# A delta-rule layer: the rescaling of the normed stream and the level masks of the triangular inverse move from GpSimd to VectorE

## The chip, the cores and the metric

The kernel runs on one core of one Trainium2 chip. The metric is device microseconds from launch to end on that core. Before the change three timed runs took 2519.2, 2519.74 and 2502.26 us; their median is 2519.2 us. A change of this kernel has to be about 1% to be told from no change.

## The reference

Two transformer blocks follow each other on 512 tokens of width 1024, in float32. The first has a windowed-attention layer (a) and a neighbourhood-attention layer (b), each with a gated feed-forward part, and ends in an RMS norm with the gain `norm_final`. The second puts 16 meta tokens in front (528 tokens from there on) and has a layer (c) with short convolutions and a gated delta rule, a layer (d) with sliding-window attention, and a feed-forward part behind each.

The change lies in layer (c). Two pieces of it matter:

- The stream that enters it: x becomes x · (row factor of the final norm) · (gain per feature). This normed x is the residual that layer (c) adds its result to.
- The delta rule, cut to its core. For each of 4 heads, tokens in chunks, k and q of 128 features, beta and the decay per token:

```
a = strictly lower part of beta * (k k^T) * decay mask
u, w = (I + a)^-1 [ v*beta , k*beta*exp(decay) ]
per chunk: v_new = u - w S ; o = q_dec S + (q k^T * decay mask) v_new ; S = S*g + k_dec^T v_new
```

## The kernel before

Tensors lie transposed, features on partitions and tokens along the free axis, 8 tiles of 128 x 528 for x. Every projection is done with float32 split into a high and a low part (`split`, L429 on ScalarE and L430 on VectorE) and three matmuls per tile (L254 to L256); its results are taken out of PSUM by VectorE (L404), which frees one of three PSUM banks named `mm`. The order of instructions on each engine isn't the order of the source: the framework's scheduler sets it when the kernel is built, and each engine then runs its list strictly in order.

Layer (c) begins with the projections of k. Behind the row factors come the convolutions (`conv_of`, three VectorE passes at L981 per tile) and `stream` (L646), which rescales the 8 tiles of x in place: per tile one multiplication by the gain on GpSimd (L652) and one by the row factor, a 128 x 512 tile r1 (L653). The rescaled tiles are then written to DRAM as the residual (`spill`). They are read back much later.

The delta rule works on 5 chunks (16 tokens, then 4 of 128). `rule` runs the preparation (`prep`) of two chunks side by side and the chain over the state behind them; `weave` interleaves this with the remaining projections of the layer (q, v, gate, z), which are the filling work for TensorE. `prep` inverts I + a by doubling: in blocks of 64, a level l takes the part of a that the mask `lev[l]` (128 x 64, made once by GpSimd) leaves, called `am`:

- level 0: `am` at L1591 on GpSimd, then x^T = identity - am at L1592 on VectorE, then a transposition on TensorE (L1605 for the upper, L1603 for the lower half), copied out by ScalarE (L1607).
- levels 1 to 5 (1 to 3 for the first chunk): `am` at L1615 on GpSimd, TensorE product with x (L1619), ScalarE copy (L1622), TensorE product (L1626), VectorE subtraction from x^T (L1627), and again the transposition.

So `am` of a level depends on `ac` (L1588) and the mask alone, not on the level before. There are 5 executions of L1591 and 23 of L1615. Other GpSimd work of the stage are the decay terms (L1523, L1551, L1557, L1559), q times the decay (L1661), the assembly of the inverse (L1636, L1638) and a sum of the output norm (L1729).

Of the kernel before, what the change touches and what calls it, by code (L numbers as in the profile page):

```python
# [13 lines left out]
ALU = mybir.AluOpType  # L14
# [5 lines left out]
S = 512  # L20
# [40 lines left out]
def bc_head(ap2, n):  # L61

    return ap2.unsqueeze(1).to_broadcast([ap2.shape[0], n, ap2.shape[1]])
# [59 lines left out]
def kernel(ctx: ExitStack, tc: tile.TileContext, stop=None, **a):  # L123
    nc = tc.nc
    V, A, G, PE = nc.vector, nc.scalar, nc.gpsimd, nc.tensor
# [15 lines left out]
    def slot(p="s"):  # L141
        for t, (n, names) in TAGS.items():
            if p in names:
                return sp.tile([P, SW], F32, tag=t, name=nm(p), bufs=n)
        return sp.tile([P, SW], F32, tag="s", name=nm(p), bufs=NSLOT)
# [7 lines left out]
    def bank(tag):  # L153
        tag, pool, bufs = psx[tag]
        return pool.tile([P, 512], F32, tag="ps" + tag, name=nm("ps" + tag), bufs=bufs)
# [48 lines left out]
    def gcol(key, k):  # L204
        return ncol[:, norm_at[key] + k:norm_at[key] + k + 1]
# [261 lines left out]
    def rows(c, cm=None):  # L467


        nw, m = c.shape[1], c.shape[2]  # L470
        rb = wk("rb")
        rv = rb[:, :nw * P].rearrange("p (w m r) -> p w m r", w=nw, m=m)
        V.tensor_copy(rv, c.unsqueeze(3).to_broadcast([P, nw, m, P // m]))
        ps = bank("s")
        for w in range(nw):
            PE.transpose(ps[:, w * P:(w + 1) * P], rb[:, w * P:(w + 1) * P], ident)
        if cm is None:
            return ps, None
        rm = tp.tile([P, P], F32, tag="rbm", name=nm("rbm"), bufs=2)
        V.tensor_copy(rm[:NMETA].rearrange("p (m r) -> p m r", m=m), cm.unsqueeze(2).to_broadcast([NMETA, m, P // m]))  # L480
        pm = bank("s")
        PE.transpose(pm[:, :NMETA], rm[:NMETA, :], ident[:NMETA, :NMETA])
        return ps, pm
# [105 lines left out]
    class FirstNorm:  # L589
# [56 lines left out]
        def stream(self, X):  # L646
            ps, _ = rows(self.y[:, 5:].unsqueeze(2))
            r1 = slot("r1")
            A.copy(r1[:, :S], ps)
            for k in range(KC):  # L650
                x = X[k][:, self.R]
                G.tensor_scalar(x, x, gcol(("norm_final", None), k), None, ALU.mult)  # L652
                G.tensor_tensor(x, x, r1[:, :S], ALU.mult)  # L653

    def load_rows_of(src, ntok, mid=None):

# [756 lines left out]
    def layer_c(X):  # L1413
# [9 lines left out]
        lev = []  # L1423
# [102 lines left out]
        def prep(c):  # L1526
            o, C = CH[c]
# [49 lines left out]
            at, ac = slot("at"), slot("ac")  # L1577
            V.tensor_tensor(at[:C, :n4], brow[:C, :n4], E[:C, :n4], ALU.mult)

            B = min(C, H)  # L1580
# [3 lines left out]
            def vb4(t, p=slice(0, C)):  # L1584
                return t[p, :4 * B].rearrange("p (h i) -> p h i", h=4)
# [2 lines left out]
                V.tensor_tensor(vb4(ac, q), v4(kk)[q, :, q], v4(at)[q, :, q], ALU.mult)  # L1588
            xt, x = slot("xt"), slot("xi")
            am = slot("am")  # L1590
            G.tensor_tensor(vb4(am), vb4(ac), bc_head(lev[0][:C, :B], 4), ALU.mult)  # L1591
            V.tensor_tensor(vb4(xt), bc_head(identc[:C, :B], 4), vb4(am), ALU.subtract)  # L1592
            if C > B:
                a2 = slot("a2")
# [3 lines left out]
            def turned(qs):  # L1598
                px = bank("s")
                for q in qs:  # L1600
                    for h in hb:
                        if q.start:
                            PE.matmul(px[q, h], xt[q, h], ident[q, q], start=True, stop=True)  # L1603
                        else:
                            PE.transpose(px[q, h], xt[q, h], ident[q, q])  # L1605
                r = slice(qs[0].start, qs[-1].stop)
                A.copy(x[r, :4 * B], px[r, :4 * B])  # L1607
# [3 lines left out]
            l = 1  # L1611
            while (1 << l) < B:
                last = (2 << l) == B
                am = slot("am")
                G.tensor_tensor(vb4(am), vb4(ac), bc_head(lev[l][:C, :B], 4), ALU.mult)  # L1615
                py = bank("s")
                for q in parts:
                    for h in hb:
                        PE.matmul(py[q, h], am[q, h], x[q, h], start=True, stop=True)  # L1619
                yield 0.8  # L1620
                y = slot("y")
                A.copy(y[:C, :4 * B], py[:C, :4 * B])  # L1622
                pzt = bank("s")
                for q in parts:
                    for h in hb:
                        PE.matmul(pzt[q, h], y[q, h], xt[q, h], start=True, stop=True)  # L1626
                V.tensor_tensor(xt[:C, :4 * B], xt[:C, :4 * B], pzt[:C, :4 * B], ALU.subtract)  # L1627
                yield 0.8
                if not last:
                    turned(parts)  # L1630
                    yield 0.43
                l += 1
# [117 lines left out]
        def rule():  # L1750
            todo, gens, nxt, ch = list(range(len(CH))), [], 0, None
            while nxt < len(CH) or after:
                while todo and len(gens) < 2:
                    if todo[0] < 2:
                        for c in range(min(2, len(CH)) if todo[0] == 0 else 0):
                            decay_rows(c)
                    else:
                        decay_rows(todo[0])
                    gens.append(prep(todo.pop(0)))
                for g in list(gens):  # L1760
                    try:
                        yield next(g)
                    except StopIteration:
                        gens.remove(g)
                for g in list(after):
                    try:
                        yield next(g)
                    except StopIteration:
                        after.remove(g)
                if ch is None and nxt in state:  # L1770
                    ch = chain(nxt)
                if ch is not None:
                    try:
                        yield next(ch)
                    except StopIteration:
                        ch = None
                        nxt += 1
# [436 lines left out]
```

## Time and profile before

| what | value |
|---|---|
| median of three runs | 2519.2 us |
| the profiled execution's own time | 2514.64 us |
| its span, first to last instruction | 2512.9 us |
| TensorE (PE) matmul busy | 2457.7 us, 98% |
| VectorE (DVE) busy | 1831.0 us, 73% |
| ScalarE (ACT) busy | 1199.2 us, 48% |
| GpSimd (POOL) busy | 278.5 us, 11% |
| granted TensorE clock, mean | 0.980 |

The granted clock is a share of 2.4 GHz; where a stretch shows 0.50, TensorE ran at 1.2 GHz. A TensorE that is busy at 0.50 does half the work in the same busy time. Layer (c) lies between about 1178 and 1530 us of the span. In the views, "idle before" names the time that an engine stood idle before an instruction and what ended that time.

### The profile page before, as it was taken

The page shows a single profiled execution, that of the slowest core. Times are in us where ns is not written, and L with a number is a line of the kernel's source. Part 1 is how long each engine was busy: PE and PEld are TensorE (multiplying, and loading weights), DVE is VectorE, ACT ScalarE, POOL GpSimd, SP SyncE. Part 2 cuts the span into 40 slices and gives each one's busy share as a digit, 9 for nine tenths or more (in the row PEclk, how much of TensorE's full clock was granted, in tenths as well). Part 3 has the DMA queues.
Part 4 walks back from the last instruction along what each step waited for, and adds up shares of the span by engine and source line. Part 5 has one row for each costly group of instructions (what it writes and reads, how often), then busy time and mean ns, then how long its engine had stood idle before and what let it go on. Part 6 is the DMA issues. An engine that isn't in the chain of part 4 may idle for free.

```text
span 2512.9 us, 44394 instructions
## 1 busy us (share of the span) xinstructions
PE 2457.7 (98%) x17518; PEld 2223.6 (88%) x17518; DVE 1831.0 (73%) x3520; ACT 1199.2 (48%) x2199; POOL 278.5 (11%) x403
## 2 busy tenths in 40 slices
PE   8999999999999999999999999999999999999999
PEld 6787789998887799998888899899999978889998
DVE  6875767778765878777836446978887776788885
ACT  4764444445555444445423224445544664445553
POOL 3120300003130200003312220200000000100000
PEclk9999999999999999999969999999999999999999
DMA  6142224344232223333311113123324312223332
GB/s 194 43 142 83 78 74 124 111 151 134 77 102 64 63 89 114 105 106 102 108 31 38 35 51 120 55 82 112 98 89 144 68 40 81 68 88 102 101 97 84
DMA packets 345445, 229.19 MB, mean 91 GB/s; under 512 B 54435, under 2 KB 335444, under 8 KB 345236
## 3 DMA queue, kind: packets, MB, share of 16 engines
q1 hardware_dynamic: 342372, 217.59, 29.3%
q0 software_dynamic: 2864, 8.77, 1.1%
q8 instruction: 137, 2.24, 0.4%
q14 instruction: 72, 0.59, 0.1%
HBM read 214.10 MB, written 13.74 MB: 91 GB/s over the span
## 4 chain that ended last, share of the span: by engine, by line
PE 44%; DVE 4%; issue 2%; POOL 1%; ACT 0%; POOLq 0%; DVEq 0%
PE mm L254 10%; PE mm L255 10%; PE mm L256 10%; PE pss L254 1%; PE pss L255 1%; PE pss L256 1%; PE pss L1619 1%; PE pso L2046 1%; PE pss L1626 1%; PE pso L254 1%; PE pso L255 1%; PE pso L256 1%; DVE xb L430 1%; PE pss L1603 1%; PE pss L2031 1%
## 5 line engine op out<-in xcount | busy, mean ns | idle before, releaser
L429 ACT ACTIVATE hi<-raw 128x1024 fp32r<-128x1024 f32 (+1 forms) x458 | 475.5, 1040 | 533.9 <-PE pss L255 256.1
L430 DVE TENSOR_TENSOR lo<-raw,hi 128x1024 fp32r<-128x1024 f32 (+1 forms) x458 | 560.1, 1224 | 135.9 <-ACT hi L429 132.5
L254 PE MATMUL mm<-xh,hi 128*128 128x264 f32 (+3 forms) x1168 | 390.1, 334 | 8.6 <-ACT xh L508 3.2
L255 PE MATMUL mm<-xl,hi 128*128 128x264 f32 (+3 forms) x1168 | 381.4, 327 | 0.6 <-DVE xl L509 0.5
L256 PE MATMUL mm<-xh,lo 128*128 128x264 f32 (+3 forms) x1168 | 379.3, 325 | 0.0
L254 PE MATMUL mm<-xb,hi 128*128 128x256 f32 (+2 forms) x1152 | 328.0, 285 | 18.5 <-ACT xb L429 8.2
L256 PE MATMUL mm<-xb,lo 128*128 128x256 f32 (+2 forms) x1152 | 328.2, 285 | 3.0 <-DVE lo L430 3.0
L255 PE MATMUL mm<-xb,hi 128*128 128x256 f32 (+2 forms) x1152 | 327.5, 284 | 0.3
L256 PE MATMUL mm<-ah,lo 128*128 128x512 f32 (+1 forms) x880 | 307.7, 350 | 0.5 <-DVE lo L430 0.5
L255 PE MATMUL mm<-al,hi 128*128 128x512 f32 (+1 forms) x880 | 307.9, 350 | 0.1
L254 PE MATMUL mm<-ah,hi 128*128 128x512 f32 (+1 forms) x880 | 307.7, 351 | 0.2
L254 PEld LDWEIGHTS mm<-xh,hi 128*128 128x128 f32 x1168 | 226.2, 194 | 32.5 <-issue 6.9
L688 DVE TENSOR_TENSOR xr<-mm,xr 128x512 f32<-128x512 f32 (+1 forms) x288 | 158.2, 557 | 128.5 <-PE mm L256 128.3
L255 PEld LDWEIGHTS mm<-xl,hi 128*128 128x128 f32 x1168 | 226.1, 194 | 17.3 <-DVE xl L509 2.4
L254 PEld LDWEIGHTS mm<-xb,hi 128*128 128x128 f32 x1152 | 219.3, 190 | 23.5 <-ACT xb L429 9.1
L256 PEld LDWEIGHTS mm<-xh,lo 128*128 128x128 f32 x1168 | 225.7, 193 | 16.2 <-issue 0.5
L256 PEld LDWEIGHTS mm<-xb,lo 128*128 128x128 f32 x1152 | 219.8, 191 | 4.0 <-DVE lo L430 3.9
L255 PEld LDWEIGHTS mm<-xb,hi 128*128 128x128 f32 x1152 | 219.2, 190 | 3.4 <-DVE xb L430 0.9
L256 PEld LDWEIGHTS mm<-ah,lo 128*128 128x128 f32 x880 | 165.4, 188 | 23.2 <-DVE lo L430 0.8
L254 PEld LDWEIGHTS mm<-ah,hi 128*128 128x128 f32 x880 | 165.3, 188 | 19.5 <-ACT ah L429 0.9
L255 PEld LDWEIGHTS mm<-al,hi 128*128 128x128 f32 x880 | 165.5, 188 | 18.8 <-DVE al L430 1.0
L255 PE MATMUL pss<-xb,hi 128*128 128x256 f32 (+2 forms) x576 | 163.3, 284 | 1.8 <-DVE xb L430 1.8
(527 smaller groups left out, 5194.1 us busy)
## 6 DMA issues: line engine op xcount, KB each, us to landing
raw<-in_w_gate_up_dram SPq DMA_DIRECT2D x140, 256.0 KB, 3.0
raw<-in_ffn_w_up_dram SPq DMA_DIRECT2D x140, 256.0 KB, 3.0
raw<-in_w_down_dram SPq DMA_DIRECT2D x40, 512.0 KB, 3.3
raw<-in_ffn_w_down_dram SPq DMA_DIRECT2D x40, 512.0 KB, 3.4
raw<-in_mix_w_in_dram SPq DMA_DIRECT2D x28, 512.0 KB, 3.7
raw<-in_w_in_b_dram SPq DMA_DIRECT2D x20, 512.0 KB, 3.7
a<-in_w_gate_up_dram SPq DMA_DIRECT2D x36, 256.0 KB, 3.3
a<-in_ffn_w_up_dram SPq DMA_DIRECT2D x36, 256.0 KB, 2.9
```

What stands on the lines that cost most here:

```text
L254: PE.matmul(ps, r32(hi), r32(xh), start=first, stop=False, skip_group_check=more)
L255: PE.matmul(ps, r32(hi), r32(xl), start=False, stop=False, skip_group_check=more)
L256: PE.matmul(ps, r32(lo), r32(xh), start=False, stop=last, skip_group_check=more)
L429: A.activation(r32(dst_h), src, AF.Copy)
L430: V.tensor_tensor(r32(dst_l), src, dst_h, ALU.subtract)
L688: V.tensor_tensor(X[j][:, o:o + n], ps[:, :n], X[j][:, o:o + n], ALU.add)
L1603: PE.matmul(px[q, h], xt[q, h], ident[q, q], start=True, stop=True)
L1619: PE.matmul(py[q, h], am[q, h], x[q, h], start=True, stop=True)
L1626: PE.matmul(pzt[q, h], y[q, h], xt[q, h], start=True, stop=True)
L2031: PE.transpose(pt[:, d:d + P], pb[:, c:c + P], ident)
L2046: PE.matmul(po[64 * hh:64 * hh + 64, b * P:(b + 1) * P], vt[b + j][:, kv * 64:kv * 64 + 64], PT[:, (2 * hh + j) * P:(2 * hh + j + 1) * P], ...
```

## The change

`stream` multiplies each tile once, on VectorE, by the gain (a scalar per partition) and by r1 in the same instruction. The mask products `am` of all levels are issued on VectorE, with the same operands. Nothing else is edited. Behind L652 the lines of the changed kernel have numbers lower by one (L653 is gone).

```diff
             for k in range(KC):
                 x = X[k][:, self.R]
-                G.tensor_scalar(x, x, gcol(("norm_final", None), k), None, ALU.mult)
-                G.tensor_tensor(x, x, r1[:, :S], ALU.mult)
+                V.scalar_tensor_tensor(x, x, gcol(("norm_final", None), k), r1[:, :S], ALU.mult, ALU.mult)
...
             am = slot("am")
-            G.tensor_tensor(vb4(am), vb4(ac), bc_head(lev[0][:C, :B], 4), ALU.mult)
+            V.tensor_tensor(vb4(am), vb4(ac), bc_head(lev[0][:C, :B], 4), ALU.mult)
             V.tensor_tensor(vb4(xt), bc_head(identc[:C, :B], 4), vb4(am), ALU.subtract)
...
                 am = slot("am")
-                G.tensor_tensor(vb4(am), vb4(ac), bc_head(lev[l][:C, :B], 4), ALU.mult)
+                V.tensor_tensor(vb4(am), vb4(ac), bc_head(lev[l][:C, :B], 4), ALU.mult)
```

The order on the engines changes with it, from where GpSimd began to rescale x (1160 us) to the end of the delta rule. Ahead of that and behind it the lists are the same.

First place, VectorE where the convolutions of k end; L404 takes a projection out of a PSUM bank. Before:

```order
L981 SCALAR_TENSOR_TENSOR qkv_12656<-cg_12492,cwcol,qkv_12656 128x525
L404 TENSOR_TENSOR cg_12699<-mm_12726,rs_12634 128x264
L404 TENSOR_TENSOR cg_12758<-mm_12759,rs_12634 128x264
L981 SCALAR_TENSOR_TENSOR qkv_12752<-cg_12699,cwcol,qkv_12752 128x527
L981 SCALAR_TENSOR_TENSOR qkv_12752<-cg_12699,cwcol,qkv_12752 128x526
L981 SCALAR_TENSOR_TENSOR qkv_12752<-cg_12699,cwcol,qkv_12752 128x525
L430 TENSOR_TENSOR lo_12894<-raw_12891,hi_12893 128x1024
L404 TENSOR_TENSOR cg_12758<-mm_12785,rs_12634 128x264
```

With the change eight passes of `stream` (now L652; the last two are shown) stand between the sixth pass of the convolutions and the next L404:

```order
L652 SCALAR_TENSOR_TENSOR xc_12374<-xc_12374,ncol,r_12669 128x512
L652 SCALAR_TENSOR_TENSOR xc_12403<-xc_12403,ncol,r_12669 128x512
L404 TENSOR_TENSOR cg_12691<-mm_12718,rs_12634 128x264
L404 TENSOR_TENSOR cg_12750<-mm_12751,rs_12634 128x264
L404 TENSOR_TENSOR cg_12750<-mm_12777,rs_12634 128x264
```

The two L404 that followed the sixth convolution pass now follow `stream`, and the third one has moved up to them, ahead of the next convolution.

Second place, VectorE at the head of the inverse of the first two chunks. Before (the products `am` are on the list of GpSimd):

```order
L1588 TENSOR_TENSOR ac_13227<-pss_13143,at_13226 16x64
L981 SCALAR_TENSOR_TENSOR qkv_13200<-cg_13049,cwcol,qkv_13200 128x526
L1592 TENSOR_TENSOR xt_13230<-lev_12449,am_13232 16x64
L981 SCALAR_TENSOR_TENSOR qkv_13200<-cg_13049,cwcol,qkv_13200 128x525
L1578 TENSOR_TENSOR at_13244<-pss_13187,E_13164 128x512
L404 TENSOR_TENSOR cg_13541<-mm_13603,rs_12634 128x264
L1588 TENSOR_TENSOR ac_13245<-pss_13186,at_13244 64x256 x2
L404 TENSOR_TENSOR cg_13668<-mm_13669,rs_12634 128x264
L1592 TENSOR_TENSOR xt_13249<-lev_12449,am_13251 128x256
L1596 TENSOR_TENSOR a_13254<-pss_13186,at_13244 64x256
L430 TENSOR_TENSOR lo_13895<-raw_13892,hi_13894 128x1024
```

With the change (L1590 is level 0's `am`, L1591 the subtraction):

```order
L1590 TENSOR_TENSOR am_13224<-ac_13219,lev_12449 16x64
L980 SCALAR_TENSOR_TENSOR qkv_13192<-cg_13041,cwcol,qkv_13192 128x525
L1591 TENSOR_TENSOR xt_13222<-lev_12449,am_13224 16x64
L404 TENSOR_TENSOR cg_13533<-mm_13595,rs_12634 128x264
L404 TENSOR_TENSOR cg_13660<-mm_13661,rs_12634 128x264
L1577 TENSOR_TENSOR at_13236<-pss_13179,E_13156 128x512
L1587 TENSOR_TENSOR ac_13237<-pss_13178,at_13236 64x256 x2
L430 TENSOR_TENSOR lo_13887<-raw_13884,hi_13886 128x1024
L1590 TENSOR_TENSOR am_13243<-ac_13237,lev_12449 128x256
L404 TENSOR_TENSOR cg_13660<-mm_13710,rs_12634 128x264
L1591 TENSOR_TENSOR xt_13241<-lev_12449,am_13243 128x256
L1595 TENSOR_TENSOR a_13246<-pss_13178,at_13236 64x256
```

One L430 and one L404 now stand between `ac` and the x^T of the 128-token chunk, beside the mask itself. On TensorE the instructions that wait for these x^T have moved back behind filling projections: from the last product of the decay (L1575, 128 x 512) to the first chunk's transposition there were 18 matmuls of projections and are 25 now; from there to the 128-token chunk's (L1605, 64x64) there were 26 and are 45.

Third place, GpSimd at the same point; before, the products `am` of all levels of the two chunks stand one behind the other:

```order
L1559 TENSOR_TENSOR E_13164<-E_13164,rk_13077 128x512
L1591 TENSOR_TENSOR am_13232<-ac_13227,lev_12449 16x64
L1591 TENSOR_TENSOR am_13251<-ac_13245,lev_12449 128x256
L1615 TENSOR_TENSOR am_13266<-ac_13227,lev_12449 16x64
L1615 TENSOR_TENSOR am_13279<-ac_13245,lev_12449 128x256
```

With the change that list goes from the decay straight to q times the decay and the assembly of the inverse:

```order
L1558 TENSOR_TENSOR E_13156<-E_13156,rk_13069 128x512
L1660 TENSOR_TENSOR qd_13585<-qkv_13035,ed_13120 128x16
L1660 TENSOR_TENSOR qd_13585<-qkv_13192,ed_13120 128x16
L1660 TENSOR_TENSOR qd_13585<-qkv_13380,ed_13120 128x16
L1660 TENSOR_TENSOR qd_13585<-qkv_13515,ed_13120 128x16
L1635 MEMSET xf_13677 64x4x64
```

So nothing on GpSimd stands any more between the decay terms and the first assembly but q times the decay.

## Rows read from the trace of the kernel before

**Rows 1.** The page: busy time by engine (us, share of the span, instructions).

```profile
PE 2457.7 (98%) x17518; PEld 2223.6 (88%) x17518; DVE 1831.0 (73%) x3520; ACT 1199.2 (48%) x2199; POOL 278.5 (11%) x403
```

**Rows 2.** Stretches: length, busy us (instructions) of each engine, granted clock, DMA.

```profile
core 0: us, PE busy (x) PEld busy (x) DVE busy (x) ACT busy (x) POOL busy (x), PEclk, DMA share, GB/s
1256.10:1304.30 48.20, 48.16 (x362) 41.19 (x363) 13.57 (x24) 8.54 (x21) 5.47 (x10) 0.50 0.08 23
1304.30:1372.60 68.30, 66.65 (x622) 59.69 (x621) 50.09 (x122) 25.82 (x63) 18.72 (x23) 1.00 0.16 48
1372.60:1379.40 6.80, 6.80 (x42) 6.09 (x40) 2.90 (x15) 1.90 (x4) 0.00 (x0) 0.50 0.00 0
1440.80:1451.10 10.30, 10.15 (x59) 9.53 (x60) 1.81 (x3) 3.96 (x9) 1.29 (x1) 0.50 0.15 51
```

**Rows 3.** Timeline of PE around the first inverse: start us, us, instruction, [idle before].

```profile
1250.38 0.25 PE L1605 MATMUL pss<-ident,xt 16*16 16x16 f32 x4 [0.93 <-DVE xt L1592]
...
1253.59 0.28 PE L254 MATMUL mm<-xh,hi 128*128 128x264 f32 x1
1253.71 0.28 PE L255 MATMUL mm<-xl,hi 128*128 128x264 f32 x1
1256.14 0.41 PE L1605 MATMUL pss<-ident,xt 64*64 64x64 f32 x4 [2.14 <-DVE xt L1592]
```

**Rows 4.** The same timeline, DVE: from `ac` to x^T of the 128-token chunk.

```profile
1251.88 0.84 DVE L1588 TENSOR_TENSOR ac<-pss,at 64x256 f32<-64x256 f32 x2
...
1253.62 2.46 DVE L1592 TENSOR_TENSOR xt<-lev,am 128x256 f32<-128x256 f32 x1 [0.44 <-POOL am L1591]
```

**Rows 5.** The same timeline, POOL.

```profile
1252.85 0.74 POOL L1591 TENSOR_TENSOR am<-ac,lev 128x256 f32<-128x256 f32 x1 [2.77 <-PE mm L256]
1253.55 4.79 POOL L1615 TENSOR_TENSOR am<-ac,lev 16x64 f32<-16x64 f32 x7
```

**Rows 6.** The chain of waits, at 1.2 and later at 2.4 GHz: start us, us, what.

```profile
1276.00 1.04 PE pss L1603 x8
1278.32 1.53 PE pss L1619 x16
...
1391.57 0.89 PE pss L1619 x16
...
1398.83 0.60 PE pss L1603 x8
```

**Rows 7.** Who waited for whom on PE, 1195 to 1450 us: total us, times, longest.

```profile
PE pss L1605 <- DVE xt L1592: 5.2, 4, 2.1
PE mm L254 <- DVE cg L404: 2.0, 2, 1.5
```

**Rows 8.** Single lines: duration ns min/median/max, first and last start, forms.

```profile
L1592 DVE TENSOR_TENSOR xt<-lev,am x5: 214/426/2458, 1250.1 to 1439.9; 128x256 f32<-128x256 f32 x4, 16x64 f32<-16x64 f32 x1
L605 DVE SCALAR_TENSOR_TENSOR xl<-xc,g,xh x8: 727/749/1095, 1156.0 to 1177.5; 128x512 fp32r<-128x512 f32 x8
L981 DVE SCALAR_TENSOR_TENSOR qkv<-cg,cwcol,qkv x36: 745/762/1804, 1195.5 to 1317.7; 128x527 f32<-128x527 f32 x12, 128x526 f32<-128x526 f32 x12, 128x525 f32<-128x525 f32 x12
```

**Rows 9.** Timeline of DVE, POOL and PE while `stream` runs.

```profile
1195.48 8.31 DVE L981 SCALAR_TENSOR_TENSOR qkv<-cg,cwcol,qkv 128x527 f32<-128x527 f32 x6
1203.72 0.76 DVE L404 TENSOR_TENSOR cg<-mm,rs 128x264 f32<-128x264 f32 x2
...
1210.11 1.21 DVE L430 TENSOR_TENSOR lo<-raw,hi 128x1024 fp32r<-128x1024 f32 x1
1211.24 0.42 DVE L404 TENSOR_TENSOR cg<-mm,rs 128x264 f32<-128x264 f32 x1
...
1196.62 13.01 POOL L653 TENSOR_TENSOR xc<-xc,r 128x512 f32<-128x512 f32 x8 [9.75 <-ACT r L649]
...
1204.19 0.39 PE L254 MATMUL mm<-xh,hi 128*128 128x264 f32 x1 [0.52 <-DVE cg L404]
```

**Rows 10.** 20 us with a short fall of the clock between dense projections.

```profile
1180.00:1200.00 20.00, 19.99 (x153) 19.58 (x152) 13.84 (x31) 6.37 (x14) 10.18 (x19) 0.91 0.45 138
```

## The prediction, as written before the changed kernel ran

> **What bounds the kernel.** I read the page first: TensorE is busy 98% of the span, GpSimd 11% [rows 1]. An engine with 11% seldom ends a run, so work taken from it gains only where something waits for it, or where TensorE's busy time is slow time. Hence the second view, the table by stretches [rows 2]: the reader is to see that TensorE is busy 48.16 of 48.20 us from 1256.1 on, but at a granted clock of 0.50 (1.2 GHz), and that this is the first inverse of the delta rule. Two more stretches of the stage, 6.8 and 10.3 us, are at 0.50 too.
>
> What did TensorE do before the clock fell? It stood idle twice, 0.93 and 2.14 us, both times for x^T of level 0 [rows 3]. The timelines of the other two engines show why [rows 4, 5]: the mask was ready at 1253.6, and then a VectorE subtraction took 2.46 us, while GpSimd ran seven masks of later levels. The same instruction takes 0.43 us as a rule [rows 8]. The same is seen at `stream`: while GpSimd multiplies 8 tiles in 13.01 us, six convolution passes take 8.31 us on VectorE, 1.39 each [rows 9], against 0.76 alone [rows 8]. So GpSimd's work isn't free though nobody waits for it in the table of waits [rows 7]: it stretches VectorE's.
>
> All times go against the profiled execution, 2514.6 us (span 2512.9). The median shown, 2519.2, is 4.6 us above it. A measurement of this kernel tells about 1% from no change, 25.2 us of that median: faster means under 2494.0, slower over 2544.4.
>
> **The change, part by part.**
>
> *The wait ahead of the first inverse.* Level 0's mask costs 0.74 us on GpSimd [rows 5]; on VectorE I price it as the subtraction of the same shape, 0.43 [rows 8]. From the end of `ac` at 1252.7 [rows 4] VectorE now runs one L430 (1.21 [rows 9]), the mask, one L404 (0.42) and the subtraction (0.43): about 2.5 us, to 1255.2, where it ended at 1256.1 before. This needs the seven masks gone from GpSimd, and the order shows that they are. TensorE meanwhile has 7 + 19 = 26 more matmuls of projections ahead of the two transpositions, 0.12 us each by their starts [rows 3]: 3.1 us of work that it would have done later. Against idle time of 3.07 us that covers all, but L430 may have to wait for ScalarE; I leave 0.9 and count **-2.2**. Bounds: -3.1 and, if all of L430 and L404 is added to the wait, +1.6.
>
> *The clock.* If TensorE doesn't stand idle there, I expect the clock to stay at 2.4 GHz. What that is worth is read from the same products at either level: 16 products L1619 take 1.53 and 0.89 us, 8 transpositions L1603 1.04 and 0.60 [rows 6], a ratio of 0.58. The stretch of 48.2 us becomes 28.0: **-20.2**. Can the dependent steps go that fast? Per level they are 0.60, twice 0.89, one subtraction of 0.43 and two copies by ScalarE that I put at 0.4: 3.6 us, five levels 18, below 28. Bounds: 0, and -20.2 - 7.2 if the other two stretches at 0.50 (17.1 us, 0.42 of it saved) go as well.
>
> *Later heads.* The other two waits for level 0 sum to 5.2 - 3.1 = 2.1 us [rows 7]; the mask is 0.3 shorter each time: **-0.6** (bounds -2.1, 0).
>
> *The other masks on VectorE.* 23 masks, 20 of them of 128x256: 20 x 0.43 + 3 x 0.21 = 9.2 us. They need `ac` alone and VectorE is busy 13.57 of 48.2 and 50.09 of 68.3 us in this part [rows 2], so I count **0**; the cover is the time in which TensorE multiplies. If every one stood ahead of a subtraction that TensorE waits for, +9.2; less than 0 isn't possible for added work, but each mask that leaves GpSimd frees VectorE too, which is counted above.
>
> *`stream` on VectorE.* Removed: 13.01 us of GpSimd and with it the stretching of nine convolution passes. Added: 8 passes, priced as the multiplication and subtraction of the same size, 0.75 [rows 8]. At 1195.5 VectorE now has 6 x 0.76 + 8 x 0.75 = 10.6 us ahead of the next L404, where it had 8.2 [rows 9]: TensorE, out of banks, waits 2.3 us longer than its 0.52. The third L404 follows at once, so the second such wait (1.5 of the 2.0 in [rows 7]) goes. Together **+0.8**; bounds -2.0 and +2.3. The residual is written out after `stream` and read much later, so its end isn't on the path. The clock may fall at this wait; what a short fall costs between dense projections is seen in [rows 10]: 20 us at 0.91, so some 1.8 us.
>
> Sum: -2.2 - 20.2 - 0.6 + 0 + 0.8 = -22.2, and 2514.6 becomes **2492**. Its own range is 2483 (both short stretches gone too) to 2503 (all masks in the way).
>
> **Rivals.**
>
> *1. The clock falls all the same.* For it: TensorE waits at several heads, and in the inverse it has few projections between small products. Two other stretches fell [rows 2], and the three runs before lie 17 us apart, about one such stretch. Against: between 1304 and 1372.6 the same mixture ran 68 us at 1.00 [rows 2]. What could keep the wait alive is the port: masks on VectorE now meet q times the decay on GpSimd, which stands right behind the decay in its list. A collision costs up to 2.46 - 0.43 = 2.0 us [rows 4, 8], and one at the head brings the wait back. Then only -2.8 + 0.8 remains, or, with part of the stretch at full clock, half of 20: 2502 to 2516, the likeliest 2512.
>
> The Trainium skill, "SBUF — State Buffer", section "SBUF: two separate sides", says that VectorE instructions with two SBUF inputs and GpSimd instructions that read SBUF share a port pair as an exclusive lock, so that the one that starts first blocks the other for its whole length. By that rule a blocked subtraction would wait for one mask, 4.79 / 7 = 0.7 us [rows 5]; the row shows about three, 2.0 us, and I price a collision by the row. By the rule a collision would be too short to bring back the wait, and the sum would stay at 2492. "Perfetto Trace Analysis", section "Optimizing Scalar/DVE Operations", draws the consequence that moving work between these two engines might not help, because of that port; here that would be this rival, 2512.
>
> *2. The masks stand in the way on VectorE, without the clock.* +9.2 as above, 2501: inside the range of the forecast, but on the "no change" side.
>
> *3. Slower: the inverse never leaves 1.2 GHz.* Place: from the first level on, the masks stand in VectorE's list ahead of the subtractions, so TensorE waits once per level; the clock falls at the head as before and, with these waits, doesn't come back at 1304.3 but only when the next pair of chunks is through at 1372.6. The projections between (1304 to 1344) are dense and would bring it back, so at most the next inverse, some 28 us, is doubled by 1 / 0.58: +20. With +9.2 for the masks and +2.3 at `stream`: 2546. It decides if two or more waits of a microsecond appear in front of L1619 or L1626 in a level. Before there was none [rows 7].
>
> That the change doesn't do what it says is out: the orders show the masks and the 8 passes on VectorE.
>
> **Numbers.** Forecast 0.58, rival 1 0.27, rival 2 0.08, rival 3 0.07. Of the forecast's 2483 to 2503 a little over 0.6 lies under 2494.0, which gives 0.36; with a few per cent from the others **faster 0.39**. **Slower 0.06**, rival 3 alone. **Same 0.55**. The range takes in the forecast's own and rival 1: **2482 to 2516**; outside are rival 3 and the tails.
>
> **What would show it.** VectorE: no L1591 (x^T) over 0.6 us and convolution passes at 0.76 while `stream` runs; the eight passes 0.75 each. TensorE: no wait over 1 us ahead of the first L1605, one of about 2 to 3 us near 1205, and the stretch of the first inverse at 1.00 and some 28 us long. Wrong would be a granted clock of 0.50 there, or waits in front of L1626. I would also be wrong if the clock stayed up and the time didn't move: then the projections, moved forward to fill the wait, are missing later.

## The result, and the profile after

The changed kernel takes **2487.16 us** (median of 4 runs, 2482.26 to 2491.49) against 2518.72 for the kernel before (4 runs): a ratio of 0.988, interval 0.9856 to 0.9904. All ratios here are taken over the single runs; they are not quotients of the medians. The profiled execution took 2484.76 us, 29.9 less than that of before.

The page: GpSimd lost 46 us, VectorE gained 3, although it now has 36 instructions more. TensorE's busy time fell by 26.6 us with the same 17518 matmuls; that is where the time came from [rows 1].

```profile
PE 2431.1 (98%) x17518; PEld 2202.7 (89%) x17518; DVE 1834.0 (74%) x3556; ACT 1199.2 (48%) x2199; POOL 232.6 (9%) x359
```

The table by stretches, after: from the first transposition of the 128-token chunk to its last subtraction, then on through the stage (length, busy us and instructions by engine, granted clock, DMA share and GB/s).

```profile
1257.15:1287.00 29.85, 29.85 (x370) 25.62 (x370) 14.10 (x32) 9.51 (x22) 0.75 (x3) 1.00 0.18 51
1287.00:1411.80 124.80, 122.68 (x1213) 111.51 (x1212) 84.28 (x217) 40.37 (x99) 24.50 (x34) 1.00 0.14 40
1411.80:1455.00 43.20, 43.20 (x445) 39.55 (x446) 23.99 (x67) 12.43 (x29) 3.76 (x6) 1.00 0.16 50
```

The same piece of the kernel before, in the same view:

```profile
1256.10:1302.70 46.60, 46.56 (x355) 39.59 (x356) 12.08 (x23) 8.54 (x21) 4.02 (x8) 0.50 0.08 24
```

The reader is to see that TensorE is busy all the time in both and that only the granted clock differs: 46.6 us at 0.50, 29.85 at 1.00, and 15 matmuls of projections more in the latter (86 instead of 71). The two later stretches at 0.50 [rows 2] are gone as well.

What stands ahead of it: the timeline of TensorE and VectorE where [rows 3] and [rows 4] were read (start us, us, instruction, idle time before).

```profile
1251.23 0.25 PE L1604 MATMUL pss<-ident,xt 16*16 16x16 f32 x4 [0.60 <-DVE xt L1591]
...
1257.17 0.41 PE L1604 MATMUL pss<-ident,xt 64*64 64x64 f32 x4
...
1260.26 0.96 PE L1618 MATMUL pss<-xi,am 64*64 64x64 f32 x16
```

```profile
1253.38 0.86 DVE L1587 TENSOR_TENSOR ac<-pss,at 64x256 f32<-64x256 f32 x2
1254.76 1.23 DVE L430 TENSOR_TENSOR lo<-raw,hi 128x1024 fp32r<-128x1024 f32 x1 [0.52 <-ACT hi L429]
1255.90 0.42 DVE L1590 TENSOR_TENSOR am<-ac,lev 128x256 f32<-128x256 f32 x1
1256.35 0.43 DVE L404 TENSOR_TENSOR cg<-mm,rs 128x264 f32<-128x264 f32 x1
1256.70 0.42 DVE L1591 TENSOR_TENSOR xt<-lev,am 128x256 f32<-128x256 f32 x1
```

Mask and subtraction take 0.42 us each; the second wait of TensorE is gone, the first is 0.60. The single lines say that this holds for all five heads, and that `stream` takes what was priced:

```profile
L1591 DVE TENSOR_TENSOR xt<-lev,am x5: 205/416/425, 1251.0 to 1411.2; 128x256 f32<-128x256 f32 x4, 16x64 f32<-16x64 f32 x1
...
L652 DVE SCALAR_TENSOR_TENSOR xc<-xc,ncol,r x8: 748/754/756, 1200.4 to 1205.1; 128x512 f32<-128x512 f32 x8
```

The timeline at `stream`, with the wait of TensorE that follows it [rows 9]:

```profile
1196.37 4.14 DVE L980 SCALAR_TENSOR_TENSOR qkv<-cg,cwcol,qkv 128x527 f32<-128x527 f32 x6
1200.43 5.39 DVE L652 SCALAR_TENSOR_TENSOR xc<-xc,ncol,r 128x512 f32<-128x512 f32 x8
1205.73 1.12 DVE L404 TENSOR_TENSOR cg<-mm,rs 128x264 f32<-128x264 f32 x3
```

```profile
1206.22 0.39 PE L254 MATMUL mm<-xh,hi 128*128 128x264 f32 x1 [1.69 <-DVE cg L404]
```

And who waited for whom on TensorE, 1195 to 1450 us, against [rows 7]:

```profile
PE mm L254 <- DVE cg L404: 1.7, 1, 1.7
PE pss L1604 <- ACT hi L429: 1.0, 1, 1.0
...
PE pss L1604 <- DVE xt L1591: 0.6, 1, 0.6
```

### The profile page after: what moved, and what is told of

It reads as the page before. It is cut to its first block, busy times and chain, and to the rows that moved or that the text cites. A ratio compares the mean times of both kernels' runs of the same rounds, so it can differ in the third digit from the quotient of the medians.

```text
span 2482.7 us, 44339 instructions
## 1 busy us (share of the span) xinstructions
PE 2431.1 (98%) x17518; PEld 2202.7 (89%) x17518; DVE 1834.0 (74%) x3556; ACT 1199.2 (48%) x2199; POOL 232.6 (9%) x359
## 3 DMA queue, kind: packets, MB, share of 16 engines
q1 hardware_dynamic: 342372, 217.59, 29.9%
## 4 chain that ended last, share of the span: by engine, by line
PE 63%; DVE 6%; issue 2%; ACT 1%; POOL 1%; POOLq 0%; ACTq 0%; DVEq 0%
PE mm L254 15%; PE mm L255 14%; PE mm L256 14%; PE pss L254 2%; PE pss L255 2%; PE pss L256 2%; PE pso L254 1%; PE pso L255 1%; DVE lo L430 1%; PE pso L256 1%; PE pso L808 1%; PE pso L2045 1%; PE pss L847 1%; DVE xb L430 1%; PE pss L798 1%
## 5 line engine op out<-in xcount | busy, mean ns | idle before, releaser
L430 DVE TENSOR_TENSOR lo<-raw,hi 128x1024 fp32r<-128x1024 f32 (+1 forms) x458 | 559.4, 1223 | 132.6 <-ACT hi L429 129.9
L254 PE MATMUL mm<-xh,hi 128*128 128x264 f32 (+3 forms) x1168 | 381.0, 327 | 7.2 <-ACT xh L508 2.3
L255 PE MATMUL mm<-xl,hi 128*128 128x264 f32 (+3 forms) x1168 | 374.1, 321 | 1.3 <-DVE xl L509 1.3
L256 PE MATMUL mm<-xh,lo 128*128 128x264 f32 (+3 forms) x1168 | 373.4, 320 | 0.0
L254 PEld LDWEIGHTS mm<-xh,hi 128*128 128x128 f32 x1168 | 220.0, 188 | 29.8 <-issue 6.7
L255 PEld LDWEIGHTS mm<-xl,hi 128*128 128x128 f32 x1168 | 220.4, 189 | 17.1 <-DVE xl L509 2.8
L256 PEld LDWEIGHTS mm<-xh,lo 128*128 128x128 f32 x1168 | 219.7, 188 | 16.2 <-issue 0.5
```

The costliest lines, as they stand in the source:

```text
L254: PE.matmul(ps, r32(hi), r32(xh), start=first, stop=False, skip_group_check=more)
L255: PE.matmul(ps, r32(hi), r32(xl), start=False, stop=False, skip_group_check=more)
L256: PE.matmul(ps, r32(lo), r32(xh), start=False, stop=last, skip_group_check=more)
L430: V.tensor_tensor(r32(dst_l), src, dst_h, ALU.subtract)
```

## The experiments

The theory: two-input products on GpSimd stretch VectorE's, x^T comes late, TensorE stands idle at the head of the first inverse, and its clock falls and stays down. The rivals: the gain comes from `stream`; or from the new order of TensorE (45 filling matmuls instead of 26), which came with the change; or the masks were late for GpSimd's own list; or the clock falls for another reason than the idle time. The "idle" column is TensorE's idle time in front of the first 64x64 transposition, "clock" the granted clock of the inverse behind it, both from the profile. Each ratio is against runs of the kernel before that were taken beside it: their medians are 2518.18 us for a to d, 2515.0 for e, g_twice, h and the change beside them, 2518.34 for g2 and i.

| kernel | median us | ratio to before (95%) | idle us | clock |
|---|---|---|---|---|
| before | 2518.72 | 1 | 2.14 | 0.50 |
| the change | 2487.16 | 0.988 (0.9856 to 0.9904) | 0 | 1.00 |
| the change, beside g, e and h | 2488.94 | 0.99 (0.9881 to 0.992) | 0 | 1.00 |
| a_stream: stream alone | 2512.56 | 0.9959 (0.9935 to 0.9983) | 2.13 | 0.50 |
| b_masks: all masks | 2490.12 | 0.989 (0.9871 to 0.9908) | 0 | 1.00 |
| c_first: level 0's mask alone | 2513.29 | 0.9989 (0.9971 to 1.0007) | 2.63 | 0.52 |
| d_later: all masks but level 0's | 2492.59 | 0.9899 (0.9881 to 0.9917) | 0 | 1.00 |
| e_fill: before, idle time filled | 2500.41 | 0.9948 (0.9929 to 0.9967) | 0 | 1.00 |
| g_twice: change, masks twice | 2491.6 | 0.9906 (0.9886 to 0.9927) | 0.42 | 1.00 |
| g2_tight: the same without gaps | 2498.03 | 0.9917 (0.9904 to 0.9931) | 1.30 | 1.00 |
| i_gaps: before, masks with gaps | 2498.08 | 0.9918 (0.9904 to 0.9931) | 0 | 1.00 |
| h_blocks: change, block sums too | 2460.28 | 0.9783 (0.9762 to 0.9804) | 0 | 1.00 |

### Which part: a_stream and b_masks

Each is one half of the diff, the other half left as it was before.

```diff
 a_stream
-                G.tensor_scalar(x, x, gcol(("norm_final", None), k), None, ALU.mult)
-                G.tensor_tensor(x, x, r1[:, :S], ALU.mult)
+                V.scalar_tensor_tensor(x, x, gcol(("norm_final", None), k), r1[:, :S], ALU.mult, ALU.mult)
 b_masks
-            G.tensor_tensor(vb4(am), vb4(ac), bc_head(lev[0][:C, :B], 4), ALU.mult)
+            V.tensor_tensor(vb4(am), vb4(ac), bc_head(lev[0][:C, :B], 4), ALU.mult)
...
-                G.tensor_tensor(vb4(am), vb4(ac), bc_head(lev[l][:C, :B], 4), ALU.mult)
+                V.tensor_tensor(vb4(am), vb4(ac), bc_head(lev[l][:C, :B], 4), ALU.mult)
```

> Only the normed stream goes to VectorE, the masks stay on GpSimd. My theory (the gain is the first inverse, whose clock falls because GpSimd's masks make x^T late): the second wait at the PSUM banks goes, a longer first one comes, within -2 to +2.3 us; the first inverse stays at a granted clock of 0.50 and the time at 2517 to 2521 us, ratio 1.000. Rival (the gain is the stream: GpSimd's 13 us of it stretched the convolutions and so moved everything behind): 2490 us, ratio 0.988.

> Only the masks go to VectorE, both passes of the normed stream stay on GpSimd. My theory: the whole gain is here; the first inverse at 1.00, some 28 us long instead of 48, time 2486 to 2492 us, ratio 0.988. Rival (the stream): 2517 to 2521 us.

The masks alone give 2490.12 us, as the theory had it. The stream alone leaves the head of the inverse as it was, within 0.01 us (TensorE, then VectorE):

```profile
1253.72 0.56 PE L1604 MATMUL pss<-ident,xt 64*64 64x64 f32 x4 [2.13 <-DVE xt L1591]
```

```profile
1251.21 2.46 DVE L1591 TENSOR_TENSOR xt<-lev,am 128x256 f32<-128x256 f32 x1 [0.44 <-POOL am L1590]
```

Its median is still 5.6 us under that of before, below the stated 2517. Nine of its 12 runs lie at 2506 to 2519 and three at 2488 to 2497; the profile is of one of the nine. What the three did was not seen, but the mean granted clock recorded with them is 0.990 to 0.992, as in runs of the change (0.987 to 0.991), and 0.977 to 0.984 with the nine: most likely the clock stayed up in their inverse. The nine alone have a median of 2513, so some 5 us less than before remain without a shown cause. In the profile the two waits at the banks, 0.52 and 1.52 us, became one of 1.66.

### Stretching or order: c_first and d_later

```diff
 c_first
-            G.tensor_tensor(vb4(am), vb4(ac), bc_head(lev[0][:C, :B], 4), ALU.mult)
+            V.tensor_tensor(vb4(am), vb4(ac), bc_head(lev[0][:C, :B], 4), ALU.mult)
 d_later
-                G.tensor_tensor(vb4(am), vb4(ac), bc_head(lev[l][:C, :B], 4), ALU.mult)
+                V.tensor_tensor(vb4(am), vb4(ac), bc_head(lev[l][:C, :B], 4), ALU.mult)
```

> Only level 0's mask goes to VectorE; the masks of levels 1 to 5 stay on GpSimd, where they now begin as soon as ac is there. On TensorE the order ahead of the first x^T becomes that of the full change (45 filling matmuls between the two transpositions instead of 26). Theory 1 (GpSimd's two-input products stretch VectorE's): the burst of masks still runs beside L430, the mask and the subtraction, these are stretched to 1.5 to 2.5 us each, x^T comes 2 us or more after its place, the clock falls and 15 us or more of the gain are lost: 2503 to 2520 us. Theory 2 (the order matters: more filling work ahead of the transposition, whatever GpSimd does): the wait is covered, the clock stays, 2486 to 2495 us.

> The masks of levels 1 to 5 go to VectorE, level 0's stays on GpSimd. On TensorE the order up to the first x^T of the 128-token chunk is that of the kernel before (26 filling matmuls between the transpositions). Theory 1 (stretching): the subtraction takes 0.43 instead of 2.46 us, x^T is there at about 1254.1 of the old time scale, where TensorE comes at 1254.0: the wait of 2.14 us goes, the clock stays at 1.00 in the first inverse, 2488 to 2500 us. Theory 2 (order): the wait and the fall of the clock stay, 2514 to 2520 us.

This pair decides. c_first has the mask that x^T needs on VectorE and the new order, and gains nothing (the interval holds 1). Its timelines, VectorE, GpSimd and TensorE:

```profile
1254.25 1.39 DVE L430 TENSOR_TENSOR lo<-raw,hi 128x1024 fp32r<-128x1024 f32 x1 [0.51 <-ACT hi L429]
1255.56 2.87 DVE L1591 TENSOR_TENSOR am<-ac,lev 128x256 f32<-128x256 f32 x1
```

```profile
1253.82 4.32 POOL L1615 TENSOR_TENSOR am<-ac,lev 128x256 f32<-128x256 f32 x6 [4.05 <-DVE ac L1588]
```

```profile
1259.28 0.41 PE L1605 MATMUL pss<-ident,xt 64*64 64x64 f32 x4 [2.63 <-DVE xt L1592]
```

The inverse behind this wait (length, busy us, granted clock as above):

```profile
1259.30:1305.00 45.70, 45.70 (x355) 38.99 (x356) 11.21 (x22) 8.14 (x21) 2.69 (x6) 0.52 0.05 13
```

The mask, 0.42 us in the change, takes 2.87; it ends at 1258.4, just behind GpSimd's six masks (1258.1). d_later has the old order and the needed mask on GpSimd, the masks that nobody waits for on VectorE, and gains nearly all:

```profile
1257.77 0.74 POOL L1591 TENSOR_TENSOR am<-ac,lev 128x256 f32<-128x256 f32 x1 [2.77 <-PE mm L256]
1258.47 0.58 POOL L1661 TENSOR_TENSOR qd<-qkv,ed 128x16 f32<-128x16 f32 x2
```

```profile
1258.55 0.43 DVE L1592 TENSOR_TENSOR xt<-lev,am 128x256 f32<-128x256 f32 x1 [0.44 <-POOL am L1591]
```

The subtraction is back at 0.43 us, and the inverse runs at 1.00:

```profile
1259.00:1289.00 30.00, 29.97 (x370) 25.61 (x371) 14.52 (x32) 9.23 (x22) 1.60 (x5) 1.00 0.13 37
```

The order is out as a cause, and so are the price of the needed mask and its place in GpSimd's list: both are here as before.

### Whether the idle time drops the clock: e_fill

```diff
-            def turned(qs):
+            def turned(qs, fill=0):
                 px = bank("s")
+                for i in range(fill):
+                    PE.matmul(px[:, :264], r32(xs[0][0][:, :P]), r32(xs[0][0][:, :264]), start=True, stop=True)
...
-            turned(parts)
+            turned(parts, 48 if c == 1 else 0)
```

> The kernel before, masks and stream on GpSimd, and ahead of the first 64x64 transposition 48 extra products of 128x264 on TensorE, whose result is overwritten; they need nothing that is late. 48 x 0.12 = 5.8 us of added work fills the place where TensorE stood idle for 2.14 us, the subtraction on VectorE stays at some 2.5 us. Theory 1 (the clock falls because TensorE stands idle there): the inverse at 1.00; 2518 + 5.8 - 2.1 - 20 = 2502 us, between 2496 and 2508. Rival (the clock falls for the small products themselves, or for something on GpSimd or VectorE): the stretch stays at 0.50 and the time is 2518 + 3.7 = 2522 us or more.

Measured: 2500.41 us, beside the 2502 that were worked out. The timeline of TensorE and that of VectorE:

```profile
1253.69 0.26 PE L1607 MATMUL pss<-ident,xt 16*16 16x16 f32 x4 [0.92 <-DVE xt L1592]
1253.87 6.09 PE L1601 MATMUL pss<-xh 128*128 128x264 f32 x48
1259.89 0.41 PE L1607 MATMUL pss<-ident,xt 64*64 64x64 f32 x4
```

```profile
1256.93 2.49 DVE L1592 TENSOR_TENSOR xt<-lev,am 128x256 f32<-128x256 f32 x1 [0.91 <-POOL am L1591]
```

The subtraction is as late as before, GpSimd does what it did, and TensorE does 6 us of work that is thrown away. The 48 products stand in for the wait and for the 26 projections that filled this place before; those now come behind the transposition. Yet the kernel is 0.52% faster, since the inverse behind it runs at 1.00:

```profile
1259.90:1290.00 30.10, 30.06 (x372) 25.73 (x372) 12.81 (x23) 9.69 (x23) 4.47 (x10) 1.00 0.13 37
```

With d_later, where nothing was added, this shows that at this place it is the idle time that costs, by the clock; the small products of this inverse don't bring the clock down by themselves. It is not the only way in which it falls. In the second inverse the clock fell without a wait, in the kernel before [rows 2, the 6.8 us from 1372.6 on] and again in b_masks, where TensorE is busy all of the 7 us ahead of it:

```profile
1350.60:1357.60 7.00, 7.00 (x103) 6.30 (x101) 5.22 (x12) 2.92 (x5) 1.68 (x1) 1.00 0.01 2
1357.60:1364.40 6.80, 6.80 (x43) 6.33 (x43) 3.94 (x9) 1.07 (x3) 0.00 (x0) 0.50 0.33 85
```

What brought it down there is open.

### What in GpSimd's work stretches: g_twice, g2_tight, i_gaps

```diff
 g_twice, behind the mask on VectorE
+                G.tensor_tensor(vb4(cs[:, 2 * P:]), vb4(ac), bc_head(lev[l][:C, :B], 4), ALU.mult)
 g2_tight, in its place
+                for i in (0, 2):
+                    G.tensor_tensor(vb4(cs[:, 2 * P:])[:, i:i + 2, :], vb4(ac)[:, i:i + 2, :], bc_head(lev[l][:C, :B], 2), ALU.mult)
 i_gaps, in the kernel before
-            am = slot("am")
+            am = state["am"] = slot("am")
...
+                if state.get("am") is not None:
+                    G.tensor_copy(am[:1, :1], state["am"][:1, :1])
+                state["am"] = am
                 G.tensor_tensor(vb4(am), vb4(ac), bc_head(lev[l][:C, :B], 4), ALU.mult)
```

> The changed kernel, and each mask of levels 1 to 5 a second time on GpSimd, into free columns of a tile of constants that nobody reads. The lists of TensorE, VectorE and ScalarE are word for word those of the changed kernel; GpSimd alone has 23 more instructions, on nobody's way. Theory 1 (two-input products on GpSimd stretch VectorE's): six of them stand behind ac again, as when only level 0's mask moved; the mask or the subtraction on VectorE takes 2 to 3 us, TensorE waits about 2 us at the first 64x64 transposition, the first inverse runs at 0.50: 2505 to 2520 us. Rival (the masks were late because they waited in GpSimd's list, and work that nobody reads costs nothing): 2484 to 2490 us, the mask 0.42 us.

**A miss.** The masks stood on GpSimd again, on lists of the other engines that had not changed, and the time was 2491.6 us, 2.7 above the change beside it (2488.94). GpSimd, then VectorE:

```profile
1252.40 7.71 POOL L1615 TENSOR_TENSOR csts<-ac,lev 128x256 f32<-128x256 f32 x7 [4.10 <-issue]
```

```profile
1254.14 0.55 DVE L1590 TENSOR_TENSOR am<-ac,lev 128x256 f32<-128x256 f32 x1
1254.72 0.43 DVE L404 TENSOR_TENSOR cg<-mm,rs 128x264 f32<-128x264 f32 x1
1255.07 0.49 DVE L1591 TENSOR_TENSOR xt<-lev,am 128x256 f32<-128x256 f32 x1
```

Now GpSimd is the one that is stretched, 1.10 us an instruction instead of 4.79 / 7 = 0.68 [rows 5]. All these products go to one place, so each waits for the one before it; in the kernel before they had places of their own and followed each other at once. It works the other way round too: the longest of these products took 2.29 us, from 1255.81 on, while VectorE ran an L430 and two masks one behind the other. Hence theory 1a (GpSimd keeps VectorE out for as long as its instructions follow each other without a gap), and two more runs:

> As the run with the masks twice (g_twice), but each second mask is issued as two halves into two columns ranges in turn, so that no GpSimd instruction has to wait for the one before it. The lists of TensorE, VectorE and ScalarE are those of the changed kernel. Theory 1a (GpSimd keeps VectorE out for as long as its instructions follow each other without a gap; in g_twice each waited for its predecessor, and VectorE came in between): the mask or the subtraction on VectorE takes 1.5 to 3 us, TensorE waits 1 us or more at the first 64x64 transposition, and with that the clock falls: 2500 to 2518 us. Theory 1b (VectorE is kept out by one instruction at a time, or only where both read the same tile): 2486 to 2494 us, no VectorE instruction of this place longer than 1.2 us.

> The kernel before, all masks and the stream on GpSimd, but each mask of levels 1 to 5 now waits for the mask before it, through a copy of one element that its product then overwrites. GpSimd has 23 instructions more; TensorE's and VectorE's lists are the same up to the first inverse. Theory 1a (gaps let VectorE in): the subtraction x^T takes at most 1.2 us instead of 2.46, TensorE waits at most 0.9 us instead of 2.14, the first inverse runs at 1.00: 2488 to 2500 us, although GpSimd does more. Theory 1b: the subtraction takes 2 us or more and the time is 2512 to 2522 us.

i_gaps came out within the numbers of 1a. All masks are on GpSimd, with 23 copies more, and the kernel is 0.8% faster than before. GpSimd and VectorE:

```profile
1255.13 0.74 POOL L1591 TENSOR_TENSOR am<-ac,lev 128x256 f32<-128x256 f32 x1 [2.77 <-PE mm L256]
1255.94 0.44 POOL L1616 COPY am<-am 1x1 f32<-1x1 f32 x1
1256.46 0.31 POOL L1618 TENSOR_TENSOR am<-ac,lev 16x64 f32<-16x64 f32 x1
```

```profile
1255.91 0.42 DVE L1592 TENSOR_TENSOR xt<-lev,am 128x256 f32<-128x256 f32 x1 [0.44 <-POOL am L1591]
```

Beside this subtraction only the copy of one element ran, so the run shows what happens when the next product is held back; that VectorE gets in between two products is seen in g_twice alone. i_gaps stays some 7 us behind b_masks (0.9918 against 0.989). For 2.8 us of them the masks now come late themselves (who waited for whom); the rest was not placed:

```profile
PE pss L1622 <- POOL am L1618: 2.8, 3, 1.9
```

g2_tight is only half a hit. Unbroken again, GpSimd stretches the subtraction to 1.46 us, just under the range of 1a, TensorE waits 1.30, but the clock does not fall there. What it lacks to the change (0.9917 against 0.99) has another reason by the waits: GpSimd's longer list makes a sum of the output norm late, 7.6 us where the change waits 0.8.

```profile
1260.73 1.46 DVE L1591 TENSOR_TENSOR xt<-lev,am 128x256 f32<-128x256 f32 x1
```

```profile
PE pss L1734 <- POOL sq L1730: 7.6, 3, 4.0
PE pss L1604 <- DVE xt L1591: 3.1, 3, 1.3
```

So it is shown that a series of GpSimd products with breaks leaves the subtraction at 0.42 to 0.49 us, and that unbroken series stretched an instruction by 1.0 (g2_tight), 2.0 (before) and 2.45 us (c_first). What sets the size between these is open, and 1a as it stands is too strong: in the kernel before the subtraction was done at 1256.08, while GpSimd's seven products went on without a gap to 1258.34 [rows 4, 5].

### The same place elsewhere: h_blocks

```diff
-        xb = Blocks(4, lb, (T - lb) // 2, "xb", G)
+        xb = Blocks(4, lb, (T - lb) // 2, "xb", V)
```

The last argument of `Blocks` is the engine that does the sums.

> The changed kernel once more, beside the other three of this call, so that they can be compared with it on the same chip: 2484 to 2490 us.

> The changed kernel, and the block sums of the feed-forward parts (L347, L360, L365, 16 times each) also on VectorE instead of GpSimd. In the changed kernel's trace TensorE waits at the first block product of the four parts 4.8, 4.3, 4.3 and 4.1 us, and the granted clock is 0.50 for 30 us around these places. Theory 1 carried over (a chain of GpSimd at 0.75, 1.3 and 1.6 us an instruction, which also stretches VectorE's, becomes 0.43, 0.7 and 0.43): half of the waits or more and a part of the 30 us at 0.50 go, 2467 to 2481 us. Rival (VectorE is 90% busy there, and three more instructions per piece make its own list late): 2485 to 2495 us.

It beats both kernels: 2460.28 us (2458.88 to 2461.34) against 2488.94 (2487.21 to 2492.35) of the change beside it, 28.7 us or 1.15% less, and 7 us under the range that was stated. One line of three, in the change and here:

```profile
L360 POOL TENSOR_TENSOR xn<-xn,xn x16: 1289/1458/2099, 257.8 to 2170.8; 128x512 f32<-128x512 f32 x8, 128x528 f32<-128x528 f32 x4, 128x516 f32<-128x516 f32 x4
```

```profile
L360 DVE TENSOR_TENSOR xn<-xn,xn x16: 680/685/704, 259.2 to 2142.3; 128x512 f32<-128x512 f32 x8, 128x528 f32<-128x528 f32 x4, 128x516 f32<-128x516 f32 x4
```

And the stretch around the first block product, in the change and here:

```profile
250.00:300.00 50.00, 45.03 (x207) 37.76 (x206) 42.83 (x63) 22.91 (x40) 20.81 (x22) 0.90 0.21 58
```

```profile
250.00:300.00 50.00, 48.71 (x252) 41.17 (x251) 47.93 (x80) 27.31 (x45) 5.38 (x10) 1.00 0.28 80
```

In the same 50 us TensorE does 252 matmuls instead of 207, at a clock of 1.00 instead of 0.90. VectorE goes from 86% to 96% busy, and TensorE's idle time still falls, from 5.0 to 1.3 us. How much is the shorter chain (1.46 to 0.69 us for this line) and how much VectorE's freedom was not separated. The mean granted clock of the profiled executions went from 0.990 (the change beside it) to 0.999; by an estimate, 0.009 of 2487 us, at most some 22 of the 28.7 us can be that.

## Why the prediction was right, step by step

**The mechanism** is shown: stretching by GpSimd (c_first, d_later), idle time, clock (e_fill). The time lies in the forecast's own range, and the changed profile has what was named for it: x^T at most 0.43 us, no wait above 1 us at the head, the inverse at 1.00 and 29.85 us long. Less its 15 extra matmuls of projections at 0.12 it is 28.1 of 46.6, a ratio of 0.60 where 0.58 was read from the products at either clock. The ends of that range are not what its terms give: from 2492.4, both short stretches make 2485 and all masks in the way 2502, where 2483 and 2503 stand; 2487.16 lies inside either way.

**The wait at the head** was -2.2; measured 3.07 to 0.60, -2.5.

**The clock** was -20.2; the piece above went from 46.6 to 28.1, -18.5, with some 0.7 for the rest of the 48.2: 1.0 less than forecast. What was put into the bound only, the two other stretches at 0.50 (another 7.2), came true as well. That the forecast's value left them out was its largest miss, though not all of it need be the change's doing: b_masks has the same masks and a stretch of 6.8 us at 0.50 (above).

**Later heads** were -0.6; the head at 1441 went from 2.01 to 0.96 us, -1.05, though the wait is now put down to ScalarE's part of a split. **The other masks** at 0: no wait in front of L1618 or L1625 appears.

**`stream`** was +0.8 and is -0.4 by the waits (2.04 to 1.66, a_stream). The step that failed is the price of 0.76 and 0.75 us for each pass in a row (a single pass does take that): six convolutions take 4.14 and eight passes 5.39, 0.69 and 0.67 each, because one instruction starts before the one ahead of it has ended. 9.5 us stood where 10.6 were counted, so the wait near 1205 is 1.69 us and not 2 to 3.

**The sum.** The stage gave more than -22.2: the last L605 starts at 1179.5 us (1177.5 before [rows 8]), the first convolution of the next feed-forward part at 1546.6 (1580.7 before), so the stage is 36.1 us shorter. The terms above with the 7.2 make 30.3; the short fall in [rows 10], which the change has not, some 1.8 (c_first, with `stream` still on GpSimd, has it not either, so it need not be the change's doing). Four us are not placed. Some 6 us went the other way, outside: in this execution the clock fell for longer at places that the change doesn't touch, such as these 10.2 us (one feed-forward part), here and in the kernel before:

```profile
286.40:296.60 10.20, 7.67 (x35) 7.09 (x34) 7.75 (x13) 4.44 (x9) 4.60 (x7) 0.50 0.29 86
```

```profile
286.40:296.60 10.20, 6.91 (x42) 6.46 (x42) 8.62 (x15) 4.74 (x9) 5.56 (x9) 0.83 0.33 95
```

In the second profile of the change the clock is 0.83 at this place as well, so this differs between executions of one kernel. So the gain inside the stage was 14 us larger than forecast, and a loss outside it, which was not foreseen, took back 6. That the profiled time, 2484.76 us, came within 8 us of 2492 is in part luck; the range was needed.

**Rival 1** (the clock falls all the same) is out for the change, but c_first is just this rival: with level 0's mask alone on VectorE the collision brings back the wait. What it feared, q times the decay, was one or two instructions of 0.2 to 0.6 us and not a series. The Trainium skill, "SBUF — State Buffer", section "SBUF: two separate sides", lets the instruction that starts first block the other for its whole length. The trace agrees that one blocks the other, but not on the length: 2.45 us in c_first, where one GpSimd product takes 0.72. The consequence that the Trainium skill draws in "Perfetto Trace Analysis", section "Optimizing Scalar/DVE Operations", that moving work between these two might not help, did not hold here for whole series: 31.6 us, and 28.7 more in h_blocks. For level 0's mask alone, c_first, it did hold: nothing was gained. **Rivals 2 and 3** are out by the waits: none stands in front of L1618 or L1625.

## What to carry to other kernels

Look at a stretch's granted clock before its busy share, and then for the idle time in front of it (not every fall here had one): a wait of 2 us cost 20 more here, and 6 us of useless matmuls in its place were a gain. Where a VectorE instruction is several times longer in one place than elsewhere, see what GpSimd does beside it; work that nobody waits for can be what makes others late. Move the series, or break it, and then look for the same series in the other stages.

## What was not expected of the hardware

- GpSimd's products held VectorE up for 1.0 to 2.45 us where they followed each other without a gap. With gaps between them VectorE took 0.42 to 0.55 us, and GpSimd was the one stretched, 0.68 to 1.10 us a product (g_twice).
- At the same place the clock fell after idle times of 2.13, 2.14 and 2.63 us and did not after 0.42 and 1.30. These are single executions; the 12 runs of a_stream lie 31 us apart, with mean clocks of 0.977 to 0.984 and of 0.990 to 0.992, so the same program may go either way. And at 1357.6 us of b_masks the clock fell with no wait ahead of it.
- Six VectorE passes of 0.75 us each took 4.14 us together, 0.69 apiece, while nothing ran on GpSimd; beside GpSimd's products 8.31 [rows 9].
